# Squares in more buffers, rotation tables on GpSimd, scales spread by a product with the identity, and an early exponential in a hybrid decoder step

## The chip, the cores and the metric

The kernel runs on one core of a Trainium2 chip. The metric is the device time of one execution in microseconds. A core has five engines with a queue each that is worked off in order: TensorE (PE) multiplies matrices, VectorE (DVE), ScalarE (ACT) and GpSimd (POOL) work on elements, and SyncE (SP) issues most transfers. They wait for one another by semaphores.

## The reference, cut to what matters

The program is one inference step of a decoder layer for 1024 prompt tokens and 8 x 4 sample tokens, in float32. The change lies where the latent attention of the prompt is prepared:

```python
u, v, cq, ckv, kpe = split_in(rms_norm(xp, g_mix[l]) @ w_in[l])
a_out, _ = chunk_gmlp(u, v, w_s[l], b_s[l], ln_v_g[l], ln_v_b[l])
ckv_n = rms_norm(ckv, g_kv_a[l])                       # 256 wide
q = mla_queries(cq, pos_p, g_q_a[l], w_uq[l], g_qk_q[l])
k, vv = mla_keys_values(ckv_n, kpe, pos_p, w_uk[l], w_uv[l], g_qk_k[l])
b_out = mla_prompt_attend(q, k, vv)                    # 8 heads, 64 + 32 columns, causal

def mla_queries(cq, pos, g_q_a, w_uq, g_qk_q):
    q = (rms_norm(cq, g_q_a) @ w_uq).reshape(n, t, MLA_HEADS, QK_HEAD)
    return qk_rope(rms_norm(q, g_qk_q), pos)           # norm per head, then rotation of 32 columns
```

Keys are made likewise from `ckv_n` and the rotated `kpe`. After it come the attention of the sample tokens over 4096 cached positions each, an output projection, attention to 256 memory tokens, and a gated FFN with a short convolution. The results are the two token streams and the new cache entries.

## The kernel before, in words

Tokens are on the free axis in phase 1, cut into three chunks `CH` (384, 384 and 288 columns; the last holds the 32 sample tokens) or nine tiles `TILES` of 128 (the ninth has 32). Each large product is computed as three products of split operands (`mm3`, L184): every operand is a rounded part `hi`, made by ACT (L190, L194), and the rest `lo`, made by DVE (L191, L197).

Phase 1 (`phase1`) makes the gMLP branch and then, from L457 on, the latents: for each chunk `c` four products of 128 rows (two for the queries, `cqh/cql`; two for keys and values). ACT squares them (L466), POOL adds the squares of two (L468), PE sums them over the partitions (`tok_sums`, L257), and DVE makes the inverse roots: three Newton steps of small instructions (`rsqrt`, L219 to L230). That gives `sq_tok` and `ck_tok`, one scale for each token, tokens on the partitions. The key latents need the scale along the free axis on all partitions: `tok_bc` (L265) makes, for each tile, a diagonal matrix `diag` on DVE (two buffers, L272) and multiplies a block of ones by it on PE (L273). DVE then scales the latents (`ckr`, L494), and ACT and DVE split them into `ckh/ckl`. `mix` normalises, transposes and stores tiles of the gMLP branch in the same stretch (L1419 to L1434).

`phase2a` makes tables for the rotation (`rope_tables`, L518: cosine and sine times the gains, for queries `tq` and for keys in `pre`), rotates the rope keys (`rope_tok` on POOL, L513 to L516) and then works on groups of two tiles (`proj_group`, L712), first for heads 0 to 3. For each tile it projects the queries (384 columns), the keys and the values (256 each) on PE. ACT copies the product out (L736, L732) and squares it into `hsq0` (queries, L742; DVE sums them per head, L743) or `hsq1` (keys, four squares with a running sum, L740). With one buffer for each of them, the next tile's squares wait until the last are summed. `norm` makes the scales of a group on DVE, POOL rotates the queries, DVE and POOL scale the keys (L765, L766). `head_prep` transposes queries and keys of a head (L789) and splits them into `qT` and `kT`.

From L618 on the heads are attended to in an order written out by hand for PE, ACT and DVE: scores (L184), a running maximum on DVE (L817), the exponential on ACT (L825), transposes (L834), products with the values (L847), a fold (L865). The groups for heads 4 to 7 and the preparations of later heads are spread over its steps. Up to that point the order on each engine is set by a planner that simulates the program; POOL and SP are planned by it there, too. Phase 2b (sample attention) is again ordered by hand. Tiles of closed pools are reused by later ones, and each waits for the tile that it replaces.

Of the kernel before, what the change touches and what calls it, by code (L numbers as in the profile page):

```python
# [5 lines left out]
F32 = mybir.dt.float32  # L6
FR = mybir.dt.float32r
I32 = mybir.dt.int32
AF = mybir.ActivationFunctionType
ALU = mybir.AluOpType  # L10
# [3 lines left out]
P = 128  # L14
# [139 lines left out]
class Net:  # L154
# [109 lines left out]

    def tok_bc(self, p, ps, r, c):  # L265

        nc = self.nc
        o, n = CH[c]
        for i, (t0, tn) in enumerate(TILES):
            if o <= t0 < o + n:  # L270
                dg = self.t(p, [P, P], F32, "diag", 2)[:tn, :tn]
                nc.vector.tensor_scalar(dg, self.ident[:tn, :tn], r[:tn, i : i + 1], None, ALU.mult)  # L272
                nc.tensor.matmul(ps[:, t0 - o : t0 - o + tn], self.ones[:tn], dg, start=True, stop=True)  # L273


    def phase1(self):
        nc, tc, I, O = self.nc, self.tc, self.I, self.O
        p = self.open("p1")
# [38 lines left out]
        def proj(w, i, n):  # L317
            t0, tn = TILES[i]
            ps = self.t(pp, [P, 512], F32, "mm", 5)[:tn, :n]
            self.mm3(ps, [(xh[:, k, t0 : t0 + tn], xl[:, k, t0 : t0 + tn]) for k in range(8)],  # L320
                     [(w[0][:, k], w[1][:, k]) for k in range(8)])
            return ps

        self.close("px")
        pl = self.open("pl")
# [35 lines left out]
        for hf in range(2):  # L361
# [10 lines left out]
            for i0, i1 in ((0, 3), (3, 6), (6, 8), (8, 9)):  # L372
                m, tn = i1 - i0, TILES[i0][1]
# [3 lines left out]
                for i in range(i0, i1):  # L377
                    ps = proj(w, i, 256)
# [5 lines left out]
                    sq = self.t(pg, [P, 4, 64], F32, "gsq", 2)[:tn]  # L384
# [20 lines left out]
            for i, (t0, tn) in enumerate(TILES):  # L405
                ps = proj(wu, i, nu)
# [4 lines left out]
            for g in range(4):  # L411
                G = hf * 4 + g
                d = slice(g * 64, g * 64 + 64)
                ps = self.t(pp, [P, 512], F32, "mm", 5)
# [42 lines left out]
        for c, (o, n) in enumerate(CH):  # L457
            sqc, ckr = [], []
            for m in range(4):
                ps = self.t(pp, [P, 512], F32, "mm", 5)[:, :n]  # L460
# [4 lines left out]
                sq = self.t(pl, [P, 512], F32, "csq", 4)[:, :384]  # L465
# [21 lines left out]
            self.rsqrt(pl, tf, tf, 1.0 / 256)  # L487
            nc.vector.tensor_tensor(t, t, rs, ALU.mult)
            nc.vector.tensor_copy(self.sq_tok[:, ct], t[:, :, 0])
            nc.vector.tensor_copy(ck_tok[:, ct], t[:, :, 1])  # L490
            t = self.t(pp, [P, 512], F32, "st", 3)[:, :n]
            self.tok_bc(pl, t, ck_tok, c)
# [25 lines left out]
    def rope_tables(self, p, cos, sin, g, name):  # L518

        nc = self.nc  # L520
        out = []
        for nm, t in (("c", cos), ("s", sin)):
            o = p[nm] if isinstance(p, dict) else self.t(p, [P, 9, 2, 16], F32, f"{name}_{nm}")
            for h in range(2):
                nc.vector.tensor_tensor(
                    o[:, :, h], t, g[:, h * 16 : h * 16 + 16].unsqueeze(1).broadcast_to([P, 9, 16]), ALU.mult
                )
            out.append(o.rearrange("p i h d -> p i (h d)"))
        return out
# [182 lines left out]
    def proj_group(self, p, pp, hf, i0, i1, s, c, tt=("tp", 4)):  # L712

        nc = self.nc
        m, tn = i1 - i0, TILES[i0][1]
        r = kk = q = None
# [7 lines left out]
        def part(i, z):  # L724
            t0, e = TILES[i][0], i - i0
            a, b = (self.cqh, self.cql) if z == 0 else (self.ckh, self.ckl)
            x = [(a[:, k, t0 : t0 + tn], b[:, k, t0 : t0 + tn]) for k in range(2)]
            w, n = ((s["wq"], 384), (s["wk"], 256), (s["wv"], 256))[z]
            ps = self.t(pp, [P, 512], F32, *tt)[:tn, :n]
            self.mm3(ps, x, w)  # L730
            if z == 2:
                nc.scalar.copy(s["v"][:, i], ps.rearrange("p (h d) -> p h d", h=4))  # L732
                return
            pv = ps.rearrange("p (h d) -> p h d", h=4)
            if z == 0 or i < 8:
                nc.scalar.copy(kk[:, e, :, :64] if z else q[:, e], pv)  # L736
            sq = self.t(p, [P, 4, n // 4], F32, f"hsq{z}")[:tn]
            if z == 1:
                for j in range(4):
                    nc.scalar.activation(sq[:, j], pv[:, j], AF.Square, accum_out=r[:, e, z, j : j + 1])  # L740
                return
            nc.scalar.activation(sq, pv, AF.Square)  # L742
            nc.vector.tensor_reduce(r[:, e, z], sq, AX.X, ALU.add)  # L743

        def norm():
# [24 lines left out]
            for e in range(m):  # L770
                s["q", i0 + e], s["k", i0 + e] = q[:, e], kk[:, e]

        qk = [lambda i=i, z=z: part(i, z) for i in range(i0, i1) for z in range(2)]
        it = norm()
        return [alloc] + qk + [lambda: next(it, 0)] * 6, [lambda i=i: part(i, 2) for i in range(i0, i1) if i < 8]

    def head_prep(self, p, pp, h, s, c):
# [1309 lines left out]
```

## Time and profile before

| | |
|---|---|
| median of 3 runs | 1964.19 us (1961.89 to 1965.83) |
| the profiled execution | 1963.94 us, of which its span is 1961.9 us |
| PE busy | 1882.0 us (96%) |
| DVE, ACT, POOL busy | 1372.2, 902.1, 705.0 us |
| granted PE clock, mean | 0.982 |
| table loads on ACT | 4, of 1.283 us each (L190, L380, L825, L1930) |

The profile gives for each instruction its engine, line and tiles, when it started and how long it took, and for idle time what ended it. The page sums this up over the span, "stretches" give the busy time of each engine between two moments, and "the granted clock" is the share of PE's full clock that the chip gave in that time. Latents are projected between about 150 and 197 us, the groups of heads 0 to 3 between 197 and 232 us, and the first score of the prompt attention starts at 235.18 us. A line of `rsqrt` or of `split` stands for many places; there the tile's name tells which.

### The profile page before, as it was taken

To read this page: it belongs to the slowest core of one execution; us is meant where nothing else is said; L and a number is where in the kernel's file an instruction comes from. 1 tells how busy PE (TensorE), PEld (TensorE's weight loads), DVE (VectorE), ACT (ScalarE), POOL (GpSimd) and SP (SyncE) were. 2 spreads that over 40 slices of the span, in tenths; PEclk is the share of its full clock that TensorE was granted. 3 is DMA by queue.
4 is the path that set the end of the run, shared out by engine and by line. 5 is a ranking of instruction groups with operands and counts; after the bars stand their busy time and mean duration, and the time that the engine had idled before them with its cause. 6 is when DMAs were issued, how large, how long until landed. Compare 5 with 4: busy or idle time off the path is not lost.

```text
span 1961.9 us, 40154 instructions
## 1 busy us (share of the span) xinstructions
PE 1882.0 (96%) x14556; PEld 1770.0 (90%) x14556; DVE 1372.2 (70%) x2949; ACT 902.1 (46%) x1880; POOL 705.0 (36%) x811
## 2 busy tenths in 40 slices
PE   5999899999999999999999998899999999999999
PEld 5999778768888989888899978899999999899999
DVE  8774867766777767777655668888888988832521
ACT  6334667666555555555533556433333333521311
POOL 5230401003544444444133015467677676100000
PEclk9999899999999999999999999899999999999999
DMA  5101100106865665654565145122222222754642
GB/s 202 50 5 49 57 1 2 61 14 184 223 181 162 176 176 170 173 166 136 172 186 180 37 152 184 40 78 79 86 66 77 88 75 90 213 171 128 200 124 66
DMA packets 130312, 229.42 MB, mean 117 GB/s; under 512 B 20449, under 2 KB 86850, under 8 KB 130114
## 3 DMA queue, kind: packets, MB, share of 16 engines
q1 hardware_dynamic: 129250, 225.81, 37.9%
q8 instruction: 115, 1.88, 0.4%
q10 hardware_dynamic: 864, 1.05, 0.2%
q14 instruction: 83, 0.68, 0.1%
HBM read 195.13 MB, written 31.66 MB: 116 GB/s over the span
## 4 chain that ended last, share of the span: by engine, by line
PE 67%; DVE 8%; issue 5%; DMA 4%; POOL 2%; ACT 1%; SPq 1%; POOLq 0%; DVEq 0%; ACTq 0%
PE s L184 14%; PE d L184 13%; PE b L184 7%; PE X L184 6%; PE F L184 6%; PE E L184 6%; PE A L184 3%; PE o L847 2%; PE tp L834 2%; PE tp L184 1%; DMA araw<-actd 1%; PE o L1277 1%; DMA cT<-cT 1%; DVE mx L1228 1%; PE tp L789 1%
## 5 line engine op out<-in xcount | busy, mean ns | idle before, releaser
L184 PE MATMUL s<-w2h,ch 128*128 128x288 f32 (+1 forms) x1024 | 305.9, 299 | 0.0
L184 PE MATMUL s<-w2h,cl 128*128 128x288 f32 (+1 forms) x1024 | 295.0, 288 | 2.8 <-POOL cl L1164 2.0
L184 PE MATMUL s<-w2l,ch 128*128 128x288 f32 (+1 forms) x1024 | 294.7, 288 | 0.0
L184 PE MATMUL d<-a,hi 128*128 128x264 f32 x1408 | 260.5, 286 | 3.4 <-DVE a L191 1.7
L184 PEld LDWEIGHTS d<-a,hi 128*128 128x128 f32 x1408 | 219.6, 189 | 5.2 <-DVE a L191 3.2
L184 PEld LDWEIGHTS s<-w2h,ch 128*128 128x128 f32 x1024 | 192.6, 188 | 19.1 <-issue 13.6
L184 PE MATMUL d<-a,lo 128*128 128x264 f32 x704 | 200.3, 285 | 0.0
L184 PEld LDWEIGHTS s<-w2h,cl 128*128 128x128 f32 x1024 | 192.4, 188 | 3.5 <-POOL cl L1164 2.3
L184 PEld LDWEIGHTS s<-w2l,ch 128*128 128x128 f32 x1024 | 192.8, 188 | 0.0
L1207 DVE TENSOR_REDUCE ss<-sq 128x16 f32<-128x1024 f32 x128 | 155.4, 1214 | 48.4 <-ACT sq L1204 48.2
L191 DVE TENSOR_TENSOR lo<-raw,hi 128x1024 fp32r<-128x1024 f32 (+1 forms) x71 | 83.3, 1174 | 131.3 <-ACT hi L190 131.2
L190 ACT CAST hi<-raw 128x1024 fp32r<-128x1024 f32 (+1 forms) x71 | 71.0, 1000 | 180.8 <-PE d L184 157.3
L1164 POOL TENSOR_TENSOR cl<-cT,ch 128x512 fp32r<-128x512 f32 x64 | 83.6, 1306 | 167.1 <-ACT ch L1160 148.5
L184 PEld LDWEIGHTS d<-a,lo 128*128 128x128 f32 x704 | 133.0, 189 | 0.0
L1204 ACT ACTIVATE sq<-s 128x512 f32<-128x512 f32 x128 | 76.6, 598 | 90.9 <-PE s L184 90.9
L1201 ACT ACTIVATE sq<-s 128x512 f32<-128x512 f32 x128 | 76.7, 599 | 82.9 <-PE s L184 82.6
L184 PE MATMUL mm<-whi,xh 128*128 128x256 f32 (+3 forms) x288 | 85.1, 297 | 11.0 <-ACT xh L194 11.0
L184 PE MATMUL mm<-whi,xl 128*128 128x256 f32 (+3 forms) x288 | 83.0, 299 | 7.1 <-DVE xl L197 7.1
L1521 POOL TENSOR_TENSOR acc<-acc,sqx 128x384 f32<-128x384 f32 (+1 forms) x42 | 45.9, 1093 | 110.8 <-ACT sqx L1520 109.8
L1825 POOL TENSOR_TENSOR lo<-s,hi 128x1024 fp32r<-128x1024 f32 x22 | 68.9, 3131 | 45.9 <-ACT hi L1824 45.9
L184 PE MATMUL mm<-wlo,xh 128*128 128x256 f32 (+3 forms) x288 | 84.9, 296 | 0.0
L1160 ACT CAST ch<-cT 128x512 fp32r<-128x512 f32 x128 | 73.5, 628 | 4.1 <-DMA cT<-cT 4.1
(656 smaller groups left out, 6194.4 us busy)
## 6 DMA issues: line engine op xcount, KB each, us to landing
cT<-cT SPq DMA_DIRECT2D x256, 160.0 KB, 2.5
ck<-ck SPq DMA_DIRECT2D x256, 144.0 KB, 3.2
raw<-w_up SPq DMA_DIRECT2D x44, 512.0 KB, 3.6
raw<-w_down SPq DMA_DIRECT2D x32, 512.0 KB, 3.8
actd<-cv SPq DMA_DIRECT2D x44, 264.0 KB, 2.2
araw<-actd SPq DMA_DIRECT2D x44, 264.0 KB, 4.0
raw<-w_down SPq DMA_DIRECT2D x16, 384.0 KB, 3.3
res<-res SPq DMA_DIRECT2D x16, 264.0 KB, 3.2
```

The lines of the kernel that those rows point to most:

```text
L184: self.nc.tensor.matmul(out, l, r, start=first and i == 0, stop=last and i == len(seq) - 1)
L190: {"act": nc.scalar.copy, "pool": nc.gpsimd.tensor_copy, "dve": nc.vector.tensor_copy}[eng](hi, src)
L191: low = lambda: nc.vector.tensor_tensor(lo, src, hi, ALU.subtract)
L834: nc.tensor.transpose(tp[:, z * P : z * P + P], u[e][:, jj * P : jj * P + P], self.ident)
L847: nc.tensor.matmul(u["o"][jj * 64 : jj * 64 + 64, c], s["v"][:, j + jj, h % 4], th[:, jj * 256 : jj * 256 + c.stop - c.start], start=j == ...
L1160: nc.scalar.copy(d["h"][:, k], src[k])
L1164: (nc.vector if k else nc.gpsimd).tensor_tensor(d["l"][:, k], src[k], d["h"][:, k], ALU.subtract)
L1201: nc.scalar.activation(sq[:, 0], ps[:, :, n0 : n0 + 256], AF.Square)
L1204: nc.scalar.activation(sq[:, 1], pt.rearrange("p (e d) -> p e d", e=2), AF.Square)
L1207: yield lambda: nc.vector.tensor_reduce(s["ss"][:, g0 : g0 + 2].rearrange("p e (z h) -> p z e h", z=2), sq.rearrange("p z e (h d) -> p z e ...
L1521: nc.gpsimd.tensor_tensor(acc, acc, sq, ALU.add)
L1825: eng.tensor_tensor(lo, src, hi, ALU.subtract)
```

## The change

`hsq0` has four buffers and `hsq1` two, where each had one. The eight products of `rope_tables` are issued on POOL. `tok_bc` makes no diagonal: the scale's column, repeated along the free axis, is the stationary operand and the identity the moving one, so that each product gives the same numbers in one step. After the scales of the first chunk, ACT takes the exponential of one column of `sq_tok` with factor 0 into a tile that nothing reads; with it comes the load of the exponential's table.

```diff
     def tok_bc(self, p, ps, r, c):
-        nc = self.nc
         o, n = CH[c]
         for i, (t0, tn) in enumerate(TILES):
             if o <= t0 < o + n:
-                dg = self.t(p, [P, P], F32, "diag", 2)[:tn, :tn]
-                nc.vector.tensor_scalar(dg, self.ident[:tn, :tn], r[:tn, i : i + 1], None, ALU.mult)
-                nc.tensor.matmul(ps[:, t0 - o : t0 - o + tn], self.ones[:tn], dg, start=True, stop=True)
+                self.nc.tensor.matmul(
+                    ps[:, t0 - o : t0 - o + tn], r[:tn, i : i + 1].broadcast_to([tn, P]), self.ident[:tn, :tn], start=True, stop=True
+                )
...
             nc.vector.tensor_copy(self.sq_tok[:, ct], t[:, :, 0])
+            if c == 0:
+                nc.scalar.activation(self.t(pl, [P, 1], F32, "exp"), self.sq_tok[:, :1], AF.Exp, scale=0.0)
             nc.vector.tensor_copy(ck_tok[:, ct], t[:, :, 1])
...
             for h in range(2):
-                nc.vector.tensor_tensor(
+                nc.gpsimd.tensor_tensor(
                     o[:, :, h], t, g[:, h * 16 : h * 16 + 16].unsqueeze(1).broadcast_to([P, 9, 16]), ALU.mult
                 )
...
-            sq = self.t(p, [P, 4, n // 4], F32, f"hsq{z}")[:tn]
+            sq = self.t(p, [P, 4, n // 4], F32, f"hsq{z}", 2 if z else 4)[:tn]
```

## The prediction

> **What bounds the kernel now.** I read the page first, for the span and the engine that carries it.
>
> ```profile
> span 1961.9 us, 40154 instructions
> PE 1882.0 (96%) x14556; PEld 1770.0 (90%) x14556; DVE 1372.2 (70%) x2949; ACT 902.1 (46%) x1880; POOL 705.0 (36%) x811
> ```
>
> TensorE (PE) is busy for 96% of the span, so a change to the other engines pays only where PE stands still or runs on a reduced clock. The change touches the end of phase 1 and the start of the prompt attention, so next I cut that place into stretches (the columns: stretch, its length, then busy us and count of instructions of each engine, the granted PE clock, DMA share and GB/s).
>
> ```profile
> 150.00:200.00 50.00, 50.00 (x339) 49.92 (x338) 26.28 (x125) 24.35 (x58) 6.23 (x10) 1.00 0.19 62
> ...
> core 0: us, PE busy (x) PEld busy (x) DVE busy (x) ACT busy (x) POOL busy (x), PEclk, DMA share, GB/s
> 197.00:210.00 13.00, 13.00 (x101) 12.96 (x100) 11.51 (x52) 9.77 (x44) 7.26 (x16) 1.00 0.43 134
> 210.00:213.50 3.50, 1.92 (x12) 1.40 (x11) 3.50 (x22) 2.81 (x14) 1.76 (x3) 1.00 0.00 0
> 213.50:217.00 3.50, 3.50 (x16) 3.50 (x15) 3.43 (x11) 2.14 (x12) 3.34 (x6) 0.51 0.01 2
> 217.00:220.40 3.40, 3.40 (x25) 2.88 (x23) 3.23 (x17) 2.42 (x13) 1.65 (x4) 1.00 0.00 0
> 220.40:223.50 3.10, 0.49 (x3) 0.49 (x4) 3.07 (x12) 1.43 (x4) 1.24 (x5) 1.00 0.17 35
> 223.50:227.00 3.50, 3.50 (x17) 3.50 (x16) 2.72 (x11) 0.87 (x2) 2.30 (x5) 0.54 0.77 247
> 227.00:232.00 5.00, 5.00 (x40) 4.17 (x38) 2.71 (x8) 3.63 (x24) 2.10 (x4) 0.98 0.03 10
> 232.00:237.30 5.30, 0.96 (x5) 0.64 (x5) 5.20 (x31) 3.70 (x15) 0.83 (x1) 1.00 0.00 0
> 237.30:247.60 10.30, 10.17 (x39) 8.95 (x39) 8.12 (x36) 5.06 (x12) 2.35 (x5) 0.51 0.01 2
> ```
>
> Until 210 us PE has no hole. Then come three, each followed by a stretch at half clock: 3.50 - 1.92 = 1.58 us of idleness and 3.50 x (1 - 0.51) = 1.7 us lost to the clock; 3.10 - 0.49 = 2.61 and 3.50 x 0.46 = 1.6; 5.30 - 0.96 = 4.34 and 10.30 x 0.49 = 5.0. Together 16.8 us, and the vector engine (DVE) is the one that is full beside them. The timeline names what ended each wait (start, length, engine, line; in brackets the idle time before it and its releaser).
>
> ```profile
> 210.99 0.38 PE L184 MATMUL mm<-w2h,ckh 128*128 128x256 f32 x1 [0.51 <-ACT hsq L742]
> 213.01 0.45 PE L184 MATMUL mm<-wqh,cqh 128*128 128x384 f32 x1 [1.07 <-ACT hsq L740]
> ...
> 217.13 0.61 PE L273 MATMUL st<-diag,ones 128*128 128x128 f32 x4
> ...
> 223.01 0.39 PE L184 MATMUL mm<-w2h,ckh 128*128 128x256 f32 x1 [2.61 <-ACT ckh L190]
> 235.18 0.33 PE L184 MATMUL s<-kTh,qTh 96*128 96x128 f32 x1 [3.13 <-ACT qTh L194]
> ```
>
> ```profile
> 210.45 0.49 ACT L742 ACTIVATE hsq<-mm 128x384 f32<-128x384 f32 x1 [2.42 <-DVE hr L743]
> 217.57 0.49 ACT L742 ACTIVATE hsq<-mm 128x384 f32<-128x384 f32 x1 [1.93 <-DVE hr L743]
> 222.53 0.86 ACT L190 CAST ckh<-ckr 128x288 fp32r<-128x288 f32 x2 [1.55 <-DVE ckr L494]
> 233.99 0.56 ACT L190 CAST kTh<-tp 96x512 fp32r<-96x512 f32 x1
> ```
>
> The first hole: ScalarE (ACT) waits 2.42 us to write the one `hsq` buffer, because DVE has not yet summed the tile before (L743), and PE runs out of PSUM tiles behind ACT. The second: PE needs the kv latents of the last chunk (`ckh`), and these hang on DVE.
>
> **Squares: `hsq0` from 1 to 4 buffers, `hsq1` from 1 to 2.** No instruction is added. ACT's waits of 2.42 and 1.93 us on L743 go, and with them the first hole and its slow stretch, at most 1.58 + 1.7 = 3.3 us. Late next is DVE itself, but L743 then only feeds the norm and no longer holds ACT and PE. In the second head half the same tiles are made under PE work without a hole: gain 0 there.
>
> ```profile
> 250.00:360.00 110.00, 108.77 (x756) 84.66 (x753) 78.87 (x307) 75.11 (x225) 15.71 (x30) 1.00 0.05 16
> ```
>
> The buffers take 3 x 1536 + 1024 = 5632 bytes more of each partition and move the tiles behind them. No row prices that. The nearest is a transfer into this pool that came late, below; I take 0, with 2.3 us either way for the range.
>
> ```profile
> POOL cmr L556 <- DMA pre<-c_causal: 2.3, 1, 2.3
> ```
>
> **Scales by a product with the identity.** Nine `diag` products leave DVE, and the matmuls keep number and shape. That a broadcast column costs nothing as the stationary operand is seen where the kernel does it already, in the rows of the FFN (L1778): its weight load takes 190 ns against the 188 of the full block of ones (the middle number).
>
> ```profile
> L273 PEld LDWEIGHTS st<-diag,ones x18: 181/188/193, 174.6 to 220.1; 128*128 128x128 f32 x16, 32*128 32x128 f32 x2
> ...
> L1778 PEld LDWEIGHTS A<-ident,hr x20: 180/190/193, 1252.5 to 1258.7; 128*128 128x128 f32 x16, 16*128 16x128 f32 x4
> ```
>
> For the first two chunks it is worth 0: PE is busy 50.00 of 50 us between 150 and 200. For the last chunk it matters.
>
> ```profile
> 213.84 0.70 DVE L490 COPY ck_tok<-lss 128x3 f32<-128x3 f32 x1
> 214.58 0.91 DVE L272 TENSOR_SCALAR diag<-ident,ck_tok 128x128 f32<-128x128 f32 x2
> 219.64 0.22 DVE L272 TENSOR_SCALAR diag<-ident,ck_tok 32x32 f32<-32x32 f32 x1
> 221.98 0.94 DVE L494 SCALAR_TENSOR_TENSOR ckr<-ckr,cols,st 128x288 f32<-128x288 f32 x2
> ```
>
> The scales stand at 214.5, but the third `diag` waits for one of two buffers and for its turn until 219.64, and L494 follows at 221.98. Without it PE can make all three columns at one visit. In the old order that visit is at 217.1, so L494 can run some 3 to 4 us earlier, and the hole of 2.61 us with its slow stretch of 1.6 goes, at most 4.2 us. Late next: `ck_tok` itself.
>
> **Rotation tables to GpSimd.** Eight products leave DVE with a wait on their transfer: 0.5 + 0.6 + 1.5 = 2.6 us and 1.2 us, just where DVE is full.
>
> ```profile
> L525 DVE TENSOR_TENSOR pre<-pre 128x144 f32<-128x144 f32 x4 | 1.5, 433 | 0.0
> L525 DVE TENSOR_TENSOR tq_s<-pre 128x144 f32<-128x144 f32 x2 | 0.6, 344 | 0.0
> L525 DVE TENSOR_TENSOR tq_c<-pre 128x144 f32<-128x144 f32 x2 | 0.5, 303 | 1.2 <-DMA pre<-rows 1.2
> ...
> L516 POOL TENSOR_TENSOR q<-rp,rp 128x128 f32<-128x128 f32 x4 | 1.9, 462 | 0.0
> ```
>
> On GpSimd (POOL) one of 144 columns lies between 0.46 (128) and 0.78 (256, next fence): about 0.5, so 8 x 0.5 = 4.0 us. Queued behind them are the rotations of keys and queries (L513 to L516). POOL is busy 19.7 of the 35 us from 197 to 232 (the sum of its column), so it takes up 4.0 us, though the first rotations come some 2 us later. DVE gains less than 3.8 us, because the two hold each other up:
>
> ```profile
> 208.44 0.78 POOL L513 TENSOR_TENSOR rp<-q,tq_c 128x256 f32<-128x256 f32 x1
> ...
> 208.39 0.15 DVE L228 TENSOR_TENSOR rqa<-rqa,rqh 128x6 f32<-128x6 f32 x1
> ...
> 208.54 0.72 DVE L228 TENSOR_TENSOR rqa<-rqa,rqh 128x16 f32<-128x16 f32 x1
> ```
>
> The same product, 0.15 us before POOL's, takes 0.72 beside it, until POOL's ends. So the bounds are 3.8 us won for DVE and 3.8 - 4.0 = 0.2 lost. I take 1.5, nearer the loss, for POOL then stands beside the long run of small DVE products (22 instructions in 210 to 213.5). It helps `ck_tok` and is no term of its own. The Trainium skill, page "SBUF — State Buffer", section "Who interferes with whom", says that a DVE instruction with two SBUF inputs and a GpSimd one that reads SBUF lock each other out for the whole instruction. The rows agree, 0.15 against 0.72; what it would do to the time is the second rival.
>
> **The exponential's table.** The load leaves the first softmax. It is the only one at L825, so the squares and copies that run between the later exponentials do not drive the table out.
>
> ```profile
> 171.98 1.34 ACT L1425 ACTIVATE csq<-a_all,mixr 128x512 f32<-128x512 f32 x2 [2.90 <-DVE mixr L230]
> ...
> L825 ACT ACT_TABLE_LOAD  x1: 1283/1283/1283, 239.6 to 239.6; - x1
> ```
>
> Early, it falls where ACT sits idle 2.90 us and PE has no hole (150 to 200): cost 0; without that cover 1.3 us of ACT. At 239.6 PE runs on other scores meanwhile (10.17 of 10.30 us busy), so of 1.28 I take 0.6, half, and keep 0 and 1.28 as ends.
>
> **Sum.** Removable are 3.3 + 4.2 = 7.5 us. Would another engine then be in the way? Over 197 to 232 PE at full clock needs 35 - 7.5 = 27.5 us, ACT has 23.1 (its column summed) and DVE 30.2 - 2.6 (tables) - 1.1 (`diag`) = 26.5, with waits inside its chains. DVE is level with PE, so I take two thirds, 5.0 us. The third hole (232 to 237) is the latency of the last tiles through norm, rotation, transposition and split; I leave it and its slow stretch as they are. 5.0 + 0.6 = 5.6 us. From 250 on PE is full again, and the later stage bound by transfers opens with a store of this one's result, queued ahead of the loads, so the gain carries:
>
> ```profile
> 452.72 0.38 SPq L1434
> ```
>
> The profiled execution took 1963.94 us (span 1961.9), 0.25 below the median of 1964.19. 1963.9 - 5.6 = 1958.3 us.
>
> By the Trainium skill, page "TensorE: Matmul & The Clock Gate", section "What's actually happening", the clock halves after an idle window of about 3.4 us. By that, holes of 1.58 and 2.61 us cost no clock, and the sum would be 4.2 x 2/3 + 0.6 = 3.4 us. The trace disagrees: after 1.58 us of idleness it grants 0.51.
>
> **Rivals.** (a) More goes than I count: ACT splits `kTh` only at 233.99, in a queue that the earlier waits have made late; if PE's wait of 3.13 us for this split goes, the third slow stretch, 10.3 us or three times the first two, can lose one of its three parts, 1.7 us. Time: 1958.3 - 4.8 = 1953.5. Against: the tail is a chain on DVE, 5.20 of 5.30 us busy.
>
> (b) GpSimd takes back what DVE was given: its eight products lock DVE for 4.0 us, DVE stays full to 224 and L494 waits there for its turn, so the second hole stays; half of the squares' 3.3 us and the table's 0.6 are left. Time: 1963.9 - 2.3 = 1961.6, no measurable change. For: the 0.72 us row. Against: it is no worse for DVE than the 3.8 us that leave. The skill's lock rule, just cited, is this one.
>
> (c) The other side: PE works in queue order, and outside the hand-ordered part a planner sets it. With no `diag` to wait for, it may place the last chunk's broadcast early, ahead of matmuls that are ready. If it stands at 207 while `ck_tok` comes at 214, PE idles 7 us and then runs three slow parts, 3 x 1.7: 12.1 us for 7.5 saved, 1968.5. It decides from a place some 4 us before the scales; nearer, it is (b). For: nothing on PE guards against it. Against: in the old trace the planner was on time (`diag` done at 215.5, PE there at 217).
>
> **How the numbers follow.** The forecast 0.45, (a) 0.15, (b) 0.21, (c) 0.19. Faster by over 0.2% (3.9 us, about what a measurement of this kernel tells from no change) is forecast and (a): 0.60; within, (b): 0.21; slower, (c): 0.19. The likeliest's own range is 1956 to 1960. The whole range reaches from (a) with the rest of the table's 1.28 and 2.3 us of moved buffers, 1950.5, to (c), 1968.5.
>
> **What would show it.** Right: no wait of ACT on L743; no ACT_TABLE_LOAD on L825, one before 175; L494 of 288 columns at 217 or sooner; granted clock 1.00 from 213 to 227; the first score on PE near 230 instead of 235.2. Wrong: a PE wait on `ck_tok` before the last broadcast; small DVE products of 0.5 us beside L525 on POOL; as much half-clock time as before, moved.

## The result, and the profile after

The changed kernel takes 1962.32 us (median of 12 runs, 1958.62 to 1965.01), the kernel before 1965.2 us beside it (12 runs, 1961.89 to 1968.38). The ratio is 0.9983 with a 95% interval of 0.9975 to 0.9991, or 3.3 us less, between 1.8 and 4.9 (the interval times 1965.2). The direction was right, and the interval keeps clear of 1. The size, forecast at 5.6 us, was too large: 0.17% lies inside the 0.2% that the prediction drew as its border, in the class that it gave to its rival (b) with a chance of 0.21. The profiled execution took 1958.62 us.

```profile
span 1956.9 us, 40156 instructions
PE 1878.0 (96%) x14556; PEld 1767.2 (90%) x14556; DVE 1374.2 (70%) x2932; ACT 901.1 (46%) x1881; POOL 707.9 (36%) x819
```

Against before, DVE has 17 instructions fewer (nine `diag`, eight for the tables) and is busy 2.0 us longer. That is the first hint. Now the stretches that the prediction cut, at the same times (length; busy us and count of PE, PEld, DVE, ACT, POOL; granted clock; DMA share; GB/s):

```profile
197.00:210.00 13.00, 13.00 (x101) 12.96 (x100) 12.52 (x57) 10.30 (x53) 8.92 (x19) 1.00 0.31 94
210.00:213.50 3.50, 2.22 (x16) 1.78 (x15) 3.43 (x12) 2.81 (x14) 3.29 (x7) 1.00 0.01 2
213.50:217.00 3.50, 3.50 (x30) 3.37 (x28) 3.23 (x11) 0.00 (x0) 2.34 (x4) 1.00 0.00 0
217.00:220.40 3.40, 1.65 (x8) 1.22 (x7) 3.40 (x9) 2.79 (x15) 2.55 (x6) 0.86 0.44 116
220.40:223.50 3.10, 3.10 (x16) 3.10 (x16) 3.00 (x11) 1.26 (x3) 2.79 (x7) 0.61 0.67 201
223.50:227.00 3.50, 3.50 (x28) 2.88 (x27) 3.29 (x14) 3.01 (x22) 2.14 (x5) 1.00 0.01 2
227.00:232.00 5.00, 1.32 (x11) 1.04 (x10) 4.86 (x24) 4.32 (x17) 0.40 (x1) 1.00 0.00 0
232.00:237.30 5.30, 3.03 (x11) 2.61 (x12) 5.23 (x22) 0.74 (x2) 1.13 (x1) 0.60 0.01 3
237.30:247.60 10.30, 10.30 (x54) 9.37 (x54) 8.20 (x33) 6.39 (x15) 1.46 (x4) 0.71 0.00 0
```

PE's holes are still there. They were 1.58, 2.61 and 4.34 us, together 8.5. Now they are 3.50 - 2.22 = 1.28, then 3.40 - 1.65 = 1.75, then 3.68 + 2.27 = 5.95 in the two stretches before 237.3, together 9.0. What the clock takes fell from 8.3 to 0.5 + 1.2 + 2.1 + 3.0 = 6.8 us (each length times one less the clock). So idleness has moved to the back rather than gone. PE's timeline of the changed kernel (start, length, engine, line; in brackets the idle time before and its releaser) names the new waits of some length:

```profile
212.57 1.04 PE L270 MATMUL st<-ident,ck_tok 128*128 128x128 f32 x6 [1.28 <-DVE ck_tok L492]
218.09 0.38 PE L184 MATMUL mm<-w2h,ckh 128*128 128x256 f32 x1 [0.86 <-ACT ckh L190]
219.48 0.58 PE L184 MATMUL mm<-w2h,ckl 128*128 128x256 f32 x1 [0.89 <-DVE ckl L191]
233.56 0.66 PE L791 MATMUL tp<-ident,k 128*96 128x128 f32 x2 [4.20 <-DVE rqa L227]
```

PE now waits for the scales (`ck_tok`, 1.28 us), as rival (c) had it, but for a fifth of the time. The latents still hold it, 0.86 and 0.89 instead of 2.61. New is the wait of 4.20 us: the transposes of the last two key tiles now stand in PE's queue ahead of the first score (233.87 us, before 235.18), where before they stood at 238.26, behind the scores of the first two query tiles. The projections end earlier all the same: the first transpose of a key is at 226.46 instead of 230.35 us. On ACT the table load and the split of the latents have moved as foreseen:

```profile
168.19 1.28 ACT L491 ACT_TABLE_LOAD   x1
...
217.61 0.43 ACT L190 CAST ckh<-ckr 128x288 fp32r<-128x288 f32 x1 [4.80 <-DVE ckr L496]
...
237.14 0.49 ACT L827 ACTIVATE prs<-prs,nm,rq 128x128 f32<-128x128 f32 x1 [2.30 <-DVE nm L823]
```

ACT's waits on the sums of the squares are gone. In their place it waits 4.80 us for DVE's scaled latents and 2.30 us for DVE's maximum. Its other long waits, 2.94 and 1.66 us, are for products and transposes of PE.

To compare kernels I cut the path at two marks that each of them has, and read their distance in one profiled execution each. The first mark is the start of the last sum over the partitions (L257), from which the last scales follow. The second is the start of POOL's product for the last two key tiles (`k<-kr,hr` of 256 columns, the last one). From there to the first product with the values (`o<-pth,v`) it is transposition, split, scores and exponential. The first part, for before and after:

```profile
203.40:236.47 33.07, 25.10 (x155) 22.92 (x154) 29.62 (x138) 20.78 (x102) 17.48 (x35) 0.90 0.12 37
```

```profile
202.60:232.37 29.77, 22.69 (x152) 20.78 (x151) 28.98 (x119) 19.57 (x96) 19.45 (x40) 0.94 0.14 40
```

Before, DVE is busy for 29.62 of 33.07 us and idle for 3.45. After, it is busy for 28.98 of 29.77 and idle for 0.79. Of the 3.3 us that this part has lost, 2.7 are DVE's idle time and 0.6 its work. DVE ran dry in the old kernel because ACT came late, and ACT because PE, after its second hole and on half clock, delivered the last tiles late. First DVE's waits there (engine, tile, line, releaser: us, times, longest), then ACT's waits for PE that stand ahead of them in its queue (ACT's timeline):

```profile
DVE wvl L191 <- ACT wvh L190: 1.9, 1, 1.9
DVE hr L743 <- ACT hsq L742: 0.6, 1, 0.6
DVE hr L750 <- ACT hsq L740: 0.4, 1, 0.4
```

```profile
225.15 0.48 ACT L736 COPY q<-mm 128x384 f32<-128x384 f32 x1 [1.76 <-PE mm L184]
228.37 0.37 ACT L736 COPY k<-mm 128x256 f32<-128x256 f32 x1 [2.35 <-PE mm L184]
```

In the changed kernel the view of DVE's waits has no row at all: DVE never waits, and so its own queue sets when the last keys are there. The second part went from 13.2 to 14.0 us. Together: 46.3 to 43.8 us, and as the first mark stands 0.8 us earlier (among the kernels below it lies anywhere from 201.8 to 204.3), the first product with the values starts at 246.4 instead of 249.7.

### The profile page after: what moved, and what is told of

It is laid out like the page before. It is cut to its first block, busy times and chain, and to the rows that moved or that the text cites. A ratio compares the mean times of both kernels' runs of the same rounds, so it can differ in the third digit from the quotient of the medians.

```text
span 1956.9 us, 40156 instructions
## 1 busy us (share of the span) xinstructions
PE 1878.0 (96%) x14556; PEld 1767.2 (90%) x14556; DVE 1374.2 (70%) x2932; ACT 901.1 (46%) x1881; POOL 707.9 (36%) x819
## 3 DMA queue, kind: packets, MB, share of 16 engines
q10 hardware_dynamic: 864, 1.05, 0.2%
## 4 chain that ended last, share of the span: by engine, by line
PE 75%; DVE 11%; issue 5%; DMA 4%; ACT 2%; POOL 2%; SPq 1%; POOLq 0%; DVEq 0%; ACTq 0%
PE s L184 15%; PE d L184 12%; PE mm L184 8%; PE X L184 6%; PE b L184 6%; PE F L184 6%; PE E L184 6%; PE A L184 3%; PE o L849 2%; PE tp L836 2%; DMA araw<-actd 1%; PE tp L184 1%; PE o L1279 1%; DVE mx L1230 1%; POOL S L1227 1%
## 5 line engine op out<-in xcount | busy, mean ns | idle before, releaser
L184 PEld LDWEIGHTS s<-w2h,ch 128*128 128x128 f32 x1024 | 193.4, 189 | 19.1 <-issue 13.6
```

The costliest lines, as they stand in the source:

```text
L184: self.nc.tensor.matmul(out, l, r, start=first and i == 0, stop=last and i == len(seq) - 1)
```

## The experiments

The theory after the result was: DVE sets the pace of the stretch, and part of what the change won before 227 us PE loses again in its queue ahead of the first scores. One rival was that GpSimd's tables take back, through the lock, what they free. The other was that a single one of the four edits makes the gain.

All kernels, with the marks as above. "To keys" is the first part, "DVE busy" DVE's busy time in it, "to values" the second part. The ratios are against the kernel before on the same chip; most kernels ran 10 to 12 times, "only product" 5 times.

| kernel | median us | ratio, 95% interval | to keys | DVE busy | to values | sum |
|---|---|---|---|---|---|---|
| before | 1965.2 | 1 | 33.1 | 29.6 | 13.2 | 46.3 |
| changed | 1962.32 | 0.9983, 0.9975 to 0.9991 | 29.8 | 29.0 | 14.0 | 43.8 |
| changed, one buffer | 1963.84 | 0.9995, 0.9985 to 1.0005 | 29.7 | 28.9 | 13.1 | 42.8 |
| changed, tables on DVE | 1960.74 | 0.9981, 0.9971 to 0.9991 | 28.7 | 28.1 | 12.3 | 41.0 |
| changed, diagonals | 1963.32 | 0.9987, 0.9977 to 0.9996 | 29.9 | 29.2 | 13.6 | 43.5 |
| changed, late table load | 1962.73 | 0.9987, 0.9978 to 0.9997 | 29.7 | 28.9 | 14.1 | 43.8 |
| only buffers | 1960.64 | 0.998, 0.997 to 0.9989 | 31.9 | 28.8 | 13.1 | 45.0 |
| only tables on GpSimd | 1962.13 | 0.9988, 0.9978 to 0.9998 | 30.4 | 29.2 | 13.2 | 43.6 |
| only product | 1959.15 | 0.9977, 0.9962 to 0.9992 | 28.0 | 27.4 | 12.3 | 40.3 |
| late groups | 1965.64 | 1.0011, 1.0002 to 1.002 | 31.2 | 28.0 | 16.9 | 48.1 |
| changed, keys behind | 1965.45 | 1.0, 0.9991 to 1.0009 | 29.4 | 28.6 | 18.1 | 47.5 |
| product, keys behind | 1963.77 | 0.9991, 0.9982 to 1.0 | 29.1 | 28.5 | 15.6 | 44.6 |
| tables on DVE, keys behind | 1963.8 | 0.999, 0.9981 to 0.9999 | 28.7 | 28.2 | 14.3 | 43.0 |
| before, keys behind | 1970.94 | 1.0028, 1.0019 to 1.0038 | 34.5 | 30.2 | 15.7 | 50.2 |

The path accounts for most of the times: what a kernel's sum differs from 46.3 us, taken as a share of 1965 us, lies within the interval of its ratio for 11 of the 13 kernels. The exceptions are one buffer (3.5 us shorter, but at most 2.9 us faster by its interval) and only buffers (1.3 us shorter, but at least 2.2 us faster).

**One buffer again.**

```diff
-            sq = self.t(p, [P, 4, n // 4], F32, f"hsq{z}", 2 if z else 4)[:tn]
+            sq = self.t(p, [P, 4, n // 4], F32, f"hsq{z}")[:tn]
```

> The changed kernel with one buffer again for each kind of squares; all else as changed. Measured on PE: the stretch from the last column sum of the latents' squares (L257, csq) to the first product with the values (o); it is 46.3 us before (203.4 to 249.7) and 43.8 after (202.6 to 246.4). If the buffers removed the first hole: two waits of ACT of about 2 us on the per-head sums come back, a PE hole of 1 to 1.6 us with a half-clock stretch near 210, and the stretch grows by 1 to 3 us over 43.8. If the chain on DVE sets the start of the attention anyway, it stays within 0.5 us of 43.8.

The path did not get longer: 42.8 us instead of 43.8, and to the last keys 29.7 as with the buffers. Yet the waits that the buffers were to remove are back, together longer than in the old kernel (ACT's timeline; 2.42 and 1.93 us there):

```profile
217.73 0.49 ACT L744 ACTIVATE hsq<-mm 128x384 f32<-128x384 f32 x1 [3.09 <-DVE hr L745]
224.55 0.49 ACT L744 ACTIVATE hsq<-mm 128x384 f32<-128x384 f32 x1 [1.62 <-DVE hr L745]
```

So these waits were a symptom: ACT stands there because DVE is late, and DVE is no less late with more buffers. A hole of PE near 210 us did not come back. The ratio, 0.9995, hints at a small loss without the buffers, but its interval overlaps that of the full change.

**Tables on DVE.**

```diff
-                nc.gpsimd.tensor_tensor(
+                nc.vector.tensor_tensor(
```

> The changed kernel with the rotation tables on DVE again. If GpSimd relieves DVE, the last chunk's scales (ck_tok) come 2 us or more later than the 212.4 us of the changed kernel and the stretch from the last csq sum to the first o grows by 1 to 2 us over 43.8. If GpSimd's products lock DVE out for as long as they take (rival b), the scales come at the same time within 0.7 us or sooner, and the stretch is 43.8 or shorter.

The path became 2.8 us shorter and the scales came 1.3 us sooner (`ck_tok` done at 211.2 instead of 212.5 us), as rival (b) has it. Of the 2.8 us, 1.1 lie before the last keys and 1.7 behind, where the planner's order changed with it: the transposes of the last two key tiles stand behind the first two score products, and DVE splits the first keys (`kTl`, 229.88 us) ahead of the last keys' scaling, not behind it (233.45, below). Why GpSimd's tables give so little is seen in the changed kernel. First POOL's timeline, then DVE's in the same microseconds (not every row):

```profile
201.29 0.96 POOL L527 TENSOR_TENSOR tq_c<-pre 128x144 f32<-128x144 f32 x2 [1.76 <-DMA pre<-rows]
202.20 0.96 POOL L527 TENSOR_TENSOR tq_s<-pre 128x144 f32<-128x144 f32 x2
203.12 1.89 POOL L527 TENSOR_TENSOR pre<-pre 128x144 f32<-128x144 f32 x4
```

```profile
201.38 0.43 DVE L230 SCALAR_TENSOR_TENSOR rqy<-rqa,rqy 32x1 f32<-32x1 f32 x1
201.84 0.42 DVE L227 TENSOR_TENSOR rqa<-rqy 32x1 f32<-32x1 f32 x1
202.19 0.53 DVE L745 TENSOR_REDUCE hr<-hsq 128x4 f32<-128x384 f32 x1
...
202.76 0.42 DVE L750 TENSOR_TENSOR hr<-hr,sq_tok 128x8 f32<-128x8 f32 x1
203.10 0.14 DVE L230 SCALAR_TENSOR_TENSOR rqy<-rqa,rqy 32x1 f32<-32x1 f32 x1
203.21 0.42 DVE L751 TENSOR_TENSOR hr<-hr,sq_tok 128x8 f32<-128x8 f32 x1
...
203.71 0.38 DVE L227 TENSOR_TENSOR rqa<-rqy 32x1 f32<-32x1 f32 x1
...
204.09 0.47 DVE L484 TENSOR_TENSOR lss<-lss,rs_tok 128x6 f32<-128x6 f32 x1
...
204.56 0.47 DVE L220 TENSOR_SCALAR rqh<-rqx 128x16 f32<-128x16 f32 x1
```

Beside the eight products of 0.47 us, seven small DVE instructions take 0.38 to 0.47 us where their like take 0.13 to 0.16: together 3.01 instead of about 1.05, so 2.0 us of DVE go to waiting for GpSimd. The products themselves took DVE 2.65 us before (0.53 + 0.61 + 1.51), so it nets 0.7, besides its wait of 1.16 us on their transfer. A sum (TENSOR_REDUCE, 0.53 us here and 0.53 to 0.55 elsewhere) is not held up. The Trainium skill, page "SBUF — State Buffer", section "Who interferes with whom", says that a sum never contends and a product of two tiles does. The trace agrees: the sum keeps its 0.53 us, while a product of two tiles takes 0.42 instead of 0.15.

**Diagonals again, and the table load late again.**

```diff
-                self.nc.tensor.matmul(
-                    ps[:, t0 - o : t0 - o + tn], r[:tn, i : i + 1].broadcast_to([tn, P]), self.ident[:tn, :tn], start=True, stop=True
-                )
+                dg = self.t(p, [P, P], F32, "diag", 2)[:tn, :tn]
+                self.nc.vector.tensor_scalar(dg, self.ident[:tn, :tn], r[:tn, i : i + 1], None, ALU.mult)
+                self.nc.tensor.matmul(ps[:, t0 - o : t0 - o + tn], self.ones[:tn], dg, start=True, stop=True)
```

> The changed kernel with the diagonal matrices on DVE again. If the third diagonal made the second hole: a PE wait of 2 us or more for the last chunk's latents (ckh) comes back with a half-clock stretch, and the stretch from the last csq sum to the first o grows by 2 to 4 us over 43.8. If the last tiles' chain through norm and transposition sets the end, the hole comes back and the stretch grows by less than 1 us.

```diff
-            if c == 0:
-                nc.scalar.activation(self.t(pl, [P, 1], F32, "exp"), self.sq_tok[:, :1], AF.Exp, scale=0.0)
```

> The changed kernel without the early exponential; nothing is left out of the result. The table load of 1.28 us comes back ahead of the first softmax. Forecast of the prediction: 0.6 us (0 to 1.28) on the stretch from the last csq sum to the first o, so 44.4. In the changed kernel ACT waits 2.30 us for DVE before the first exponential; if the load fits into that wait, the stretch stays at 43.8 within 0.2.

Both come out with the changed kernel: 43.5 and 43.8 us against 43.8, ratios of 0.9987 with intervals that overlap that of the change. With the diagonals PE's hole before the latents is back, 1.64 us long (at 222.18), but without a slow stretch behind it, and the path does not grow. The late table load is hidden, as ACT's timeline of that kernel shows: it ends at 236.84, and ACT still waits 0.99 us for DVE.

```profile
235.56 1.28 ACT L824 ACT_TABLE_LOAD   x1
237.83 0.49 ACT L824 ACTIVATE prs<-prs,nm,rq 128x128 f32<-128x128 f32 x1 [0.99 <-DVE nm L820]
```

**Each edit alone, on the kernel before** (the edits are those of the change).

```diff
+            sq = self.t(p, [P, 4, n // 4], F32, f"hsq{z}", 2 if z else 4)[:tn]
```

> The kernel before with the change's buffers for the squares alone. Stretch from the last csq sum (L257) to the first product with the values (o): 46.3 us before. By the prediction's term ACT's two waits on the per-head sums and the first PE hole go, two thirds of 3.3 us: 44.1. If ACT's wait only moves to DVE's later steps, the first hole goes and the stretch stays within 1 us of 46.3. In this kernel's PE queue the last keys' transposes stand ahead of the first score, as in the changed kernel; if that order is what costs, PE waits some 3 to 4 us there.

```diff
+                nc.gpsimd.tensor_tensor(
```

> The kernel before with the rotation tables on GpSimd alone. If the lock between GpSimd and DVE takes back what DVE is given (rival b), the stretch from the last csq sum to the first o is 46.3 within 1 us or longer, and ck_tok of the last chunk comes at 213 to 215. If DVE is relieved (the forecast), ck_tok comes 1.5 us earlier and the stretch is 44.5 to 45.5.

```diff
+                self.nc.tensor.matmul(
+                    ps[:, t0 - o : t0 - o + tn], r[:tn, i : i + 1].broadcast_to([tn, P]), self.ident[:tn, :tn], start=True, stop=True
+                )
```

> The kernel before with the product with the identity alone. By the prediction's term the second hole and its half-clock stretch go, two thirds of 4.2 us: a stretch of 43.5 from the last csq sum to the first o. If the second hole is refilled by another wait, 45.5 to 46.5.

The path gets shorter by 1.3, 2.7 and 6.0 us. The buffers bring less than the 2.2 us expected, the tables more than the 0.8 to 1.8 us of a relieved DVE and against rival (b), the product more than twice its 2.8 us. The times fall by 0.20, 0.12 and 0.23%, in sum 0.55%, where all of them together bring 0.17%: the gains do not add. The buffers alone are the plainest case. ACT's waits on L743 are gone, and PE has the same two holes as before, the first in one piece of 1.80 us (before, 0.51 + 1.07). First PE's timeline, then ACT's:

```profile
213.01 0.54 PE L184 MATMUL mm<-wqh,cqh 128*128 128x384 f32 x1 [1.80 <-ACT hsq L740]
223.03 0.39 PE L184 MATMUL mm<-w2h,ckh 128*128 128x256 f32 x1 [2.65 <-ACT ckh L190]
```

```profile
211.19 0.72 ACT L1425 ACTIVATE csq<-a_all,mixr 32x512 f32<-32x512 f32 x1 [2.86 <-DVE mixr L230]
```

ACT stands 2.86 us at its next instruction that needs DVE, a normalisation of another branch, and PE runs out of tiles behind it as before. DVE still is idle for 3.1 us on the way to the last keys. That this kernel is measured 0.2% faster all the same is not explained by the path: its profiled execution, 1964.83 us, was the slowest of its ten.

With the product alone, DVE never runs dry, and it has the least work of all on the way to the last keys:

```profile
204.30:232.27 27.97, 22.06 (x153) 20.05 (x153) 27.42 (x130) 19.59 (x96) 18.06 (x34) 0.95 0.15 42
```

In this part the edit itself takes 1.1 us from DVE (three `diag`), and DVE's idle time falls by 2.9 of the 5.1 us to the last keys. But the part also holds less work for another reason: the table products, which before lie almost wholly behind the first mark (2.06 us of DVE), now stand ahead of it (0.20 us remain). That goes with the second chunk of latents, at 190 to 199 us. There the third `diag` waited for its buffer, and DVE scaled the latents at 197.26 us, 6.1 us before the first mark; with the product they are scaled 9.3 us before it. First DVE's timeline of the kernel before, then that of the product alone:

```profile
194.21 0.29 DVE L272 TENSOR_SCALAR diag<-ident,ck_tok 128x128 f32<-128x128 f32 x1 [3.42 <-PE st L273]
...
197.26 1.14 DVE L494 SCALAR_TENSOR_TENSOR ckr<-ckr,cols,st 128x384 f32<-128x384 f32 x2 [0.25 <-PE st L273]
```

```profile
194.99 1.14 DVE L494 SCALAR_TENSOR_TENSOR ckr<-ckr,cols,st 128x384 f32<-128x384 f32 x2 [3.98 <-PE st L271]
```

The same split, 6.1 to 6.2 us against 9.3, runs through all kernels with and without the diagonals. Where the tables are on DVE, 1.98 to 2.06 us of them lie behind the mark with the diagonals, and 0.20 to 0.66 without. So the tables on GpSimd meet another case in company than alone. Without the diagonals they would cost DVE 0.3 us behind the mark (tables on DVE), while on GpSimd five of the seven held instructions, 1.4 us too long together, lie behind it. Alone, with the diagonals, they take 0.4 us of work off DVE's 29.6, and its idle time falls by 2.3: the second hole is 1.63 us long instead of 2.61, and no slow stretch follows it.

The ratio of the product alone, 0.9977, is the lowest, but its interval holds that of the whole change. No kernel here can be called faster than the changed one. The rival of the single edit is answered thus: the product alone reaches the gain, the changed kernel without it (diagonals) has the gain all the same within the noise, so no edit is the only one that makes it.

**The last norms behind the first scores.** The tables are on DVE here; the norms of the last two groups, the splits of the weights for heads 4 to 7 and the preparation of the last keys stand in the hand-written order behind the first scores.

```diff
+        norms = []
         for g in groups:
-            for f in sum(self.proj_group(p, pp, 0, *g, st[0], c, ("mm", 5)), []):
+            qk, v = self.proj_group(p, pp, 0, *g, st[0], c, ("mm", 5))
+            if g[0] >= 6:
+                norms.append(qk[-6:])
+                qk = qk[:-6]
+            for f in qk + v:
                 f()
...
                 for e in range(2):
                     u["a"](e)
+                for f in norms[0] if u is units[0] else []:
+                    f()
...
+            k1()
+            q1()
+            for f in norms[1]:
+                f()
+            st[1].update(self.proj_weights((pm, [P, 512], F32, "pth", 5), 1))
```

> The changed kernel with the rotation tables on DVE, and with the norms of the last two groups, the split of the second head half's weights and the second half of head 0's transposes moved behind the scores of the first units, in the hand-written order. If the last keys' chain in front of the first score is what costs (PE's wait of 4.2 us in the changed kernel), the first score starts 3 us or more sooner after the last csq sum than the 25.5 us of the run with tables on DVE, the half-clock stretch behind it is shorter, and the stretch to the first o falls from 41.0 to 38 or less; the time falls to some 1957. If DVE's work as a whole sets the end, the moved steps come back as waits behind the first scores and the stretch stays at 40.5 to 41.5.

The first score came at 229.0 us, 25.0 us after the first mark and so hardly sooner than the 25.5 us with the tables on DVE alone, and then PE waited for DVE (its waits from 225 to 255 us):

```profile
PE s L184 <- DVE pr L832: 4.5, 1, 4.5
PE s L184 <- ACT qTh L194: 3.6, 2, 2.7
PE tp L804 <- DVE prs L832: 1.9, 1, 1.9
```

The path became 48.1 us long and the kernel 0.1% slower than before, which neither expectation had. DVE's work was only put off, and then stood in the way of the maxima that the scores need.

**The last transposes behind the first scores**, with nothing else moved, in four kernels.

```diff
-        for f in self.head_prep(pm, pp, 0, st[0], c):
-            f()
+        k0, k1, q0, q1 = self.head_prep(pm, pp, 0, st[0], c)
+        k0()
+        q0()
...
             for u in units[:2]:
                 for e in range(2):
                     u["a"](e)
                 for e in range(2):
                     u["e"](e)
+            k1()
+            q1()
```

> The changed kernel, in which head 0's transposes of the last four key tiles and of the last four query tiles are written behind the scores of the first two units instead of being placed by the planner; no operation is added or removed. Theory 'place': the new wait of 4.20 us, in which the first scores stand queued behind transposes that are not ready, is what eats the gain; then the stretch from the last sum of csq to the first value product falls from 43.8 us by about the 3 us that the kernels with the other place show (to 40 to 41.5), and the time by as much against the changed kernel, to a ratio near 0.997. Theory 'chain': the chain on DVE and GpSimd to the last keys sets the end, and the place in the queue only shows where PE waits for it; then the stretch stays at 43 to 45 us and the ratio at 0.998 to 0.999.

> The product with the identity alone, with the same transposes written behind the first two units. In the product alone the planner had them behind two score products already and the stretch was 40.3 us, so both theories expect it within 1 us of that, and a ratio of 0.997 to 0.998. If it comes out at 43 us or more, one execution of 40.3 was luck of the order elsewhere, and the product alone is worth no more than the other edits.

> The changed kernel with the tables' eight products back on DVE and the same transposes written behind the first two units. With the planner's place the stretch was 41.0 us. Against the first kernel of this call only the engine of the eight products differs, with the order of the last transposes now the same in both: if it is GpSimd's tables that cost, this one is shorter by about 2.8 us in the stretch; if the 2.8 us came from the planner's place, the two agree within 1 us.

> The kernel before with nothing changed but the place of the same transposes, behind the first two units' scores. 'Place': there they stood behind two of the first scores already, so the stretch stays near 46.3 us (45 to 47) and the ratio at 1.000. If it falls by 2 us or more, the place of these transposes alone is worth as much as the whole change.

All four got longer than with the planner's own order, by 3.7, 4.3, 2.0 and 3.9 us, and the control, the kernel before, is 0.28% slower. So the theory that the place of the transposes eats the gain falls, and the other one did not foresee the 47.5 us either. In this order, too, the product by itself is worth 5.6 us of path (50.2 to 44.6) and 0.37% of time, with intervals that do not touch. The 44.6 us lie above the 43 from which the expectation would call the 40.3 luck, but the control lost as much by the same order, so the product's 6.0 us do not hang on the planner's order. PE's timeline of the changed kernel with the transposes behind shows what takes their place:

```profile
228.86 0.48 PE L184 MATMUL s<-kTh,qTh 96*128 96x128 f32 x1 [3.83 <-ACT qTh L194]
232.98 0.47 PE L184 MATMUL s<-kTl,qTh 96*128 96x128 f32 x1 [3.64 <-DVE kTl L191]
```

The first score starts 5.0 us earlier than in the changed kernel, at 228.86, but its second part needs the low half of the first keys (`kTl`), and in DVE's queue that stands behind the scaling of the last keys. It did so in the changed kernel, too (DVE's timeline there):

```profile
232.35 0.68 DVE L767 TENSOR_TENSOR k<-k,hr 128x512 f32<-128x512 f32 x1
...
233.45 0.67 DVE L191 TENSOR_TENSOR kTl<-tp,kTh 96x512 fp32r<-96x512 f32 x1
```

So the wait of 4.20 us cost the changed kernel almost nothing: without it PE would have waited for `kTl` until 234. The place that the traces point to is that one, on DVE. In the pair with PE's order fixed by hand (the changed kernel, and the one with its tables on DVE), the second is better by 0.7 us to the last keys and by 3.8 behind them, and there DVE makes `kTl` ahead of the last keys (POOL's product of them starts at 231.32 us, in the first at 231.18):

```profile
230.34 0.68 DVE L191 TENSOR_TENSOR kTl<-tp,kTh 96x512 fp32r<-96x512 f32 x1
```

So the pairs do not show the lock's price by itself: 0.7 to 1.1 us before the last keys can be the lock's, and the rest goes with DVE's order. The ratios, 1.0 and 0.999, have intervals that overlap. That order on DVE was seen in the traces and not changed by itself, so what it is worth stays open. Over the kernels with the planner's own order, those with `kTl` ahead (before, one buffer, tables on DVE, only tables, only product) have 12.3 to 13.2 us to values, the others 13.1 to 14.1. In these kernels the place of the last transposes on PE goes with it, in the same groups; only the pair above has one PE order and two DVE orders.

## Why the prediction was right or wrong

**Direction.** It was right for the reason given: the stretch between the last sums and the first scores got shorter, and the later stages kept most of it. The first product with the values is 3.3 us earlier in the profiles, the first score of the sample attention 2.3 us (449.3 for 451.6), the end 5.0 us, and 3.3 us in the ratio. That the first and the last of these agree is chance: they are one execution each against medians, and behind 449 us the kernels' profiled executions differ by up to 6.9 us among themselves.

**Squares, at most 3.3 us.** ACT's waits on L743 went as said, and the slow stretch of 1.7 us from 213.5 went. But "L743 no longer holds ACT and PE" failed as a reason: with the buffers alone PE's first hole is 1.80 us long, and without them the changed kernel loses nothing that the path shows. Its ratio without them, 0.9995, and that of the buffers alone, 0.998, point the other way, and that stays open. What the buffers remove is the first wait on DVE in ACT's queue, and the next one, on DVE's `mixr`, is as long (2.86 us).

**Product, at most 4.2 us.** The mechanism was right: L496 with 288 columns starts at 217.07 instead of 221.98, 4.9 us earlier, where 3 to 4 were forecast. The hole went from 2.61 us to 1.28 + 0.86 + 0.89, the first of these being the wait on `ck_tok` that rival (c) described; it cost 1.3 us, not the 7 of that rival. By itself this edit is measured at 4.5 us (0.23% of 1965), of the size of the term before the factor of two thirds, and at 6.0 us of path. "For the first two chunks it is worth 0" was wrong: PE is full there, but DVE scales the second chunk 3.1 us earlier against the first mark, and with the tables on DVE 1.9 us of its work move ahead of that mark.

**Tables on GpSimd, 1.5 us for DVE between 3.8 and -0.2.** The net of 0.7 us and the wait of 1.16 make 1.8 us, close to the estimate, and the first rotation of queries comes 2.6 us later (211.08 for 208.44), where 2 were said. Alone, on the kernel before, it takes 2.7 us off the path. In the company of the other edits it helps nothing that the path shows: with the tables back on DVE it is 2.8 us shorter, of which 1.7 go with the planner's order. Rival (b) had this mechanism, and it holds for 2.0 of the 2.65 us; but the rest of (b), that DVE keeps the scaling of the latents late, did not happen. So the time fell into its class only in part for its reason.

**Table load, 0.6 us.** In the company of the other edits it measured 0, the lower end; alone it was not run. The term failed for a reason that the row of the old kernel hid: in it the first exponential follows the load at once (240.85 us, with the maximum ready at 238.91), but when the scores come earlier, ACT waits for DVE's maximum longer than the load takes (2.30 us).

**Two thirds of 7.5.** "DVE is level with PE" was the step that was mis-sized. 26.5 us were worked out for DVE in 197 to 232. In the changed kernel it is busy 12.52 + 3.43 + 3.23 + 3.40 + 3.00 + 3.29 + 4.86 = 33.7 of these 35 us: the work that left was replaced by the same instructions, held up by GpSimd, and by work of the last tiles that now come early enough. DVE is not level with PE, it is the bound from the last sums to the last keys. What the change could win there is the time in which DVE was idle, 3.45 us, and its own lost work; it won 2.7 and 0.6.

**The third hole, left as it is.** It grew, 4.34 to 5.95 us. PE reached it 3.9 us earlier (first transposes at 226.46 for 230.35), but the low half of the first keys, for which the scores wait, came only 1.8 us earlier (233.45 for 235.28), as the planner now has it on DVE behind the last keys. The first score is 1.3 us earlier, and the sum had no term for it. Part comes back behind: the first exponential is 3.7 us earlier (237.14 for 240.85) and the first product with the values 3.3.

**Signs.** Seen as foreseen: no wait on the sums, the load at 168.19, L496 at 217. Not seen: a clock of 1.00 up to 227 (0.61 from 220.4), a first score near 230 (233.87). All three signs of "wrong" came in small: the wait on `ck_tok`, the DVE products of 0.38 to 0.47 us, and half-clock time moved to the back.

The size of 5.6 us is thus two thirds too high. Half clock lost 1.5 us less than before instead of the 3.3 that two slow stretches hold, and the table's 0.6 did not exist. Nor is every slow stretch of PE worth its 1.7 us. With one buffer, the changed kernel has the same two short holes before the latents, 0.86 and 0.88 us, but no slow stretch behind them (below); the last keys come after 29.7 us, with the slow stretch after 29.8. The kernel before with its keys behind lacks the first slow stretch of the old kernel, and its last keys come no sooner (34.5 us for 33.1). At these places DVE is full and PE's clock costs the path nothing that shows, while the sum counted both stretches in full before its factor of two thirds.

## What to carry to other kernels

Before buffers are added for a waiting engine, ask what its next instruction waits for: if it is the same late engine, the wait only moves. A gain on the engine that waits is bounded by the idle time of the engine that sets the pace, here DVE's 3.45 us, beside the work that the edit takes off that engine, and that is read from its own row between two marks on the path. Edits that shorten the same wait do not add (three of these four 0.55% singly, all four 0.17% together), so each is best measured alone first. Where one engine is full, an edit can still let another run ahead: look at that engine before such a stretch is priced at 0, as the second chunk was here.

## What the runs showed of the chip

After single holes of PE of 1.28 us (212.57, changed kernel), 1.63 and 1.64 us (at 221.33 with only the tables on GpSimd, and at 222.18 with the diagonals) and 1.72 us (at 209.53, product with keys behind), the granted clock stayed at 1.00. After holes of 1.80 and 2.65 us (only the buffers) it fell to one half. The length of the idleness does not decide it alone, for two short holes in a row did both. After 0.86 and 0.89 us from 217.2 to 219.5 the clock fell in the changed kernel, and after 0.88 and 0.88 with the late table load; after 0.86 and 0.88 with one buffer it stayed, and after 0.88 and 0.88 with the changed kernel's keys behind. After 0.51 and 1.07 us it fell in the old kernel, after 0.47 and 1.06 with its keys behind it stayed. The windows of the changed kernel and of the one with one buffer, behind the same pair of holes:

```profile
219.40:222.80 3.40, 3.32 (x12) 3.32 (x13) 3.30 (x12) 1.74 (x6) 3.35 (x7) 0.50 0.75 197
```

```profile
220.70:224.10 3.40, 3.36 (x25) 3.36 (x26) 3.30 (x11) 1.83 (x6) 3.33 (x7) 1.00 0.84 204
```

The slow stretch behind such a hole is 3.4 us long. The Trainium skill, page "TensorE: Matmul & The Clock Gate", section "What's actually happening", has a free-running window of 3.413 us after which the clock changes. The trace agrees on that length, and not on the need of a whole idle window: holes of 1.75 us in two pieces were enough. That the same holes end both ways, though in different kernels, would fit a window that does not start with them; where it starts, no row here shows. So an edit should not be credited with a slow stretch that one execution lacks.
